# A decoder block on one core: spreading the norms' inverse roots, halving seven accumulating loads, moving two value products

## The chip, the core and the metric

The kernel runs on one core of one Trainium2 chip. The metric is the device time of one execution in microseconds, the median of several runs. A core has five engines that work side by side: TensorE (PE) for matrix products, VectorE (DVE), ScalarE (ACT) and GpSimd (POOL) for work on elements, and SyncE (SP), which here only issues DMAs. Each engine takes its own instructions strictly in order. The loading of a product's stationary operand is shown as an engine of its own, PEld. Data lies in an on-chip memory of 128 partitions; products are written into an accumulation memory, of which this kernel uses eight banks of 128 x 512 fp32.

## What is computed

One decoder block on 512 positions of 1024 channels, in fp32 (cut to what matters here):

```python
def rmsnorm(x, g):
    return x * lax.rsqrt(jnp.mean(x * x, axis=-1, keepdims=True) + EPS) * g

h = rmsnorm(x, norm1_g)
a_b, a_c, a_x, q, kc, vc, ksl, vsl, kwn, vwn, g_nsa, g_merge = split(h @ w_in)
y_a = a_b * causal_dwconv(a_c * a_x, conv_a_w)          # short gated convolution, 512 channels
y_b = nsa(rope(rmsnorm(q)), ...)                        # 8 heads, 2 key groups, 4 blocks of 128 queries
gm = sigmoid(g_merge)                                   # 2 x 1024 columns
x = x + (gm[..., :1024] * (y_a @ w_a_out) + gm[..., 1024:] * (y_b @ w_b_out)) @ w_o
h = rmsnorm(x, norm2_g)
gu = h @ w_ffn_in                                       # 2 x 2816 columns
x = x + (silu(causal_dwconv(gu[..., :2816]) + b) * gu[..., 2816:]) @ w_ffn_out
```

`nsa` is attention with three branches (compressed, selected and window keys), each with its own softmax and gate.

## The kernel before

**Layout.** Channels lie on partitions and the 512 positions along the free axis. A product of 1024 input channels is a chain of products over eight tiles of 128 channels, into one bank.

**Split products.** Every large product is made of three: an operand is cast to fp32r (`hi`) and the remainder kept in a second fp32r tile (`lo`). `dense` (L431) first walks over the channel tiles with hi times hi (L434) and hi weight times lo input (L435), and then a second time over them with the lo weight times the hi input (L437). So for eight tiles there are sixteen "hi" products and, behind them, eight "lo" products; the lo half of the weight is not needed before the seventeenth.

**Weights.** `load_w` (L136) fetches a weight tile of 128 x 1024 (512 KB) through SP into `raw`; ACT casts it to `hi`. The remainder is made in one of three ways. By DVE or POOL it is a subtraction (L147). By "dma" (`dma_split`, L168) ACT writes the negated cast into `lo` (L171), and POOL then issues a DMA that fetches the same weights a second time and adds them to `lo` on the way (L172). `conv_tile` (L776) makes the short convolution's three projections for four channel tiles, twelve loads; seven of them go by "dma". The tile is `wl_a` in the trace. The feed-forward part loads its tiles the same way: `wl_s` (512 KB), `tl` (256 KB), and `wl_d` (512 KB, in pieces).

**Norms.** `row_scales` (L395) makes the mean square of every position as a column per 128 positions, POOL takes the power -1/2 (`r_n`, 128 x 4), and PE spreads it over all partitions (`pr_n`, one bank), from where ACT copies it to `rb_n`. For norm 1 DVE builds a diagonal matrix `dg_n` for each of the four groups of positions and PE multiplies it by a tile of ones, four fp32 products of 128 columns (L412). For norm 2 the column itself is spread against the identity, again four fp32 products (L416).

**Attention.** `attend(pt_, g, qt)` handles one of two key groups `g` and one of four query blocks `qt`; the blocks go from `qt` 3 down to 0, each with group 0 and then group 1. Score products (`sc`, L659 and L660) go to three rotating banks; DVE takes the maximum, ACT the exponential with its sum (L713, an ACTIVATE and a read of the accumulator), and four scaled tiles `e` are turned by a DMA to DRAM (`td_e`) and one back (`tn_e`). Then ACT casts a key tile's part (`ph`, L743), POOL makes the remainder (L744), and PE multiplies the values by both (L746, L751) into `po`. The first product of a block, key tile 0 of branch 1, opens `po`.

**Gates.** `gate_tile` (L799) is a `dense` of the gate weights into `pg`; there are sixteen of them, and they are woven between the attention's products. Tiles are loaded with POOL's subtraction.

**Order.** The instructions are written in program order and then ordered on each engine by a planner that simulates the engines. `behind(later, earlier)` (L226) gives it one ordering condition between two instructions, with no wait of its own on the chip. Engine queues are then fixed.

## Time and profile before

| what | value |
|---|---|
| time, median of 3 runs | 698.46 us (697.29 to 698.58) |
| the profiled execution's own time | 699.54 us |
| its span, first to last instruction | 697.8 us |
| granted TensorE clock over the span | 1.000 of full speed |
| PE busy | 690.3 us, 99% |
| weight loads (PEld) busy | 615.4 us, 88% |
| DVE busy | 509.2 us, 73% |
| ACT busy | 436.7 us, 63% |
| POOL busy | 245.1 us, 35% |
| chain that ended last, by engine | PE 87%, DMA 6%, ACT 2%, POOL 2% |

The profile is of one execution. 1.74 us of its time lie outside the span. Times in rows are counted from the span's start. A product's busy time is modelled as longer than the distance between two starts, since products overlap; distances between starts show the rate. In a row, the bracket gives the idle time of that engine just before and what ended it.

### The profile page before, as it was taken

The page shows a single profiled execution, that of the slowest core. Times are in us where ns is not written, and L with a number is a line of the kernel's source. Part 1 is how long each engine was busy: PE and PEld are TensorE (multiplying, and loading weights), DVE is VectorE, ACT ScalarE, POOL GpSimd, SP SyncE. Part 2 cuts the span into 40 slices and gives each one's busy share as a digit, 9 for nine tenths or more (in the row PEclk, how much of TensorE's full clock was granted, in tenths as well). Part 3 has the DMA queues.
Part 4 walks back from the last instruction along what each step waited for, and adds up shares of the span by engine and source line. Part 5 has one row for each costly group of instructions (what it writes and reads, how often), then busy time and mean ns, then how long its engine had stood idle before and what let it go on. Part 6 is the DMA issues. An engine that isn't in the chain of part 4 may idle for free.

```text
span 697.8 us, 11271 instructions
## 1 busy us (share of the span) xinstructions
PE 690.3 (99%) x4123; PEld 615.4 (88%) x4123; DVE 509.2 (73%) x890; ACT 436.7 (63%) x776; POOL 245.1 (35%) x240
## 2 busy tenths in 40 slices
PE   9999999999999999999999999999999999999997
PEld 8999878878888887888889999999999999999986
DVE  6987975766576646376887999888787777877544
ACT  7635754768898877534776776666466665556530
POOL 4151432467888867552012221211112221112110
PEclk9999999999999999999999999999999999999999
DMA  7333686576776555573587977978977979875665
GB/s 264 116 97 121 159 185 142 143 249 203 250 225 214 172 175 151 179 244 100 141 194 169 234 179 190 224 178 200 221 173 173 213 179 213 184 175 108 133 138 151
DMA packets 56615, 124.87 MB, mean 179 GB/s; under 512 B 5232, under 2 KB 20976, under 8 KB 56560
## 3 DMA queue, kind: packets, MB, share of 16 engines
q1 hardware_dynamic: 35648, 79.39, 35.2%
q0 software_dynamic: 13840, 32.51, 27.4%
q10 hardware_dynamic: 7072, 12.26, 5.7%
q8 instruction: 32, 0.52, 0.3%
q14 instruction: 23, 0.19, 0.1%
HBM read 111.55 MB, written 12.58 MB: 178 GB/s over the span
## 4 chain that ended last, share of the span: by engine, by line
PE 87%; DMA 6%; ACT 2%; POOL 2%; issue 1%; DVE 1%; SPq 0%; POOLq 0%; ACTq 0%
PE p L435 10%; PE p L434 10%; PE p L437 10%; PE pdn L435 6%; PE pdn L434 6%; PE pdn L437 6%; PE pg L434 3%; PE pg L435 3%; PE pg L437 3%; DMA tn_e<-td_e 2%; PE po L435 2%; PE po L434 2%; PE po L437 2%; DMA wl_a<-in_w_a_dram 2%; PE pa L437 2%; PE pa L434 2%
## 5 line engine op out<-in xcount | busy, mean ns | idle before, releaser
L434 PE MATMUL p<-xf_h,sh 128*128 128x256 f32 x336 | 80.9, 276 | 0.0
L435 PE MATMUL p<-xf_l,sh 128*128 128x256 f32 x336 | 80.8, 276 | 0.0
L172 POOL DMA_DIRECT2D wl_s<-in_w_ff_dram x22 | 19.4, 883 | 165.4 <-ACT wl_s L171 151.5
L435 PE MATMUL pdn<-al,wh_d 128*128 128x512 f32 (+1 forms) x176 | 68.5, 389 | 0.0
L434 PE MATMUL pdn<-ah,wh_d 128*128 128x512 f32 (+1 forms) x176 | 68.2, 389 | 0.0
L164 ACT ACTIVATE sh<-s 128x1024 fp32r<-128x1024 f32 x44 | 46.4, 1056 | 27.5 <-PE p L435 26.6
L434 PEld LDWEIGHTS p<-xf_h,sh 128*128 128x128 f32 x336 | 63.1, 188 | 0.1
L435 PEld LDWEIGHTS p<-xf_l,sh 128*128 128x128 f32 x336 | 63.1, 188 | 0.1
L165 DVE TENSOR_TENSOR sl<-s,sh 128x1024 fp32r<-128x1024 f32 x44 | 53.5, 1217 | 10.7 <-ACT sh L164 10.7
L170 ACT ACTIVATE wh_s<-wr_s 128x1024 fp32r<-128x1024 f32 x22 | 23.3, 1060 | 57.1 <-PE pdn L435 53.4
L744 POOL TENSOR_TENSOR tn_e<-tn_e,ph 128x512 fp32r<-128x512 f32 x40 | 51.2, 1297 | 16.8 <-ACT ph L743 16.7
L172 POOL DMA_DIRECT2D wl_d<-in_w_dn_dram x22 | 26.4, 1200 | 74.7 <-ACT wl_d L171 73.5
L437 PE MATMUL p<-xf_h,sl 128*128 128x256 f32 x336 | 52.3, 276 | 0.0
L434 PE MATMUL pg<-xg_h,wh_g 128*128 128x512 f32 x128 | 50.2, 392 | 0.0
L435 PE MATMUL pg<-xg_l,wh_g 128*128 128x512 f32 x128 | 50.1, 392 | 0.0
L437 PE MATMUL pdn<-ah,wl_d 128*128 128x512 f32 (+1 forms) x176 | 47.5, 388 | 0.0
L437 PEld LDWEIGHTS p<-xf_h,sl 128*128 128x128 f32 x336 | 44.8, 188 | 0.2
L1098 DVE TENSOR_TENSOR x<-x,pdn 128x512 f32<-128x512 f32 x47 | 32.0, 681 | 16.6 <-PE pdn L437 16.0
L147 POOL TENSOR_TENSOR wl_g<-wr_g,wh_g 128x1024 fp32r<-128x1024 f32 x16 | 38.5, 2407 | 10.3 <-ACT wh_g L145 10.2
L435 PE MATMUL p<-xf_l,wh_s 128*128 128x256 f32 x168 | 40.4, 276 | 0.0
L434 PE MATMUL p<-xf_h,wh_s 128*128 128x256 f32 x168 | 40.4, 277 | 0.0
L437 PEld LDWEIGHTS pdn<-ah,wl_d 128*128 128x128 f32 x176 | 33.0, 188 | 6.8
(367 smaller groups left out, 2096.7 us busy)
## 6 DMA issues: line engine op xcount, KB each, us to landing
wr_s<-in_w_ff_dram SPq DMA_DIRECT2D x44, 512.0 KB, 5.4
wl_s<-in_w_ff_dram POOLq DMA_DIRECT2D x22, 512.0 KB, 7.7
wr_d<-in_w_dn_dram ACTq DMA_DIRECT2D x22, 512.0 KB, 8.0
wl_d<-in_w_dn_dram POOLq DMA_DIRECT2D x22, 512.0 KB, 9.2
wr_g<-in_w_gate_dram SPq DMA_DIRECT2D x16, 512.0 KB, 4.2
wr_a<-in_w_a_dram SPq DMA_DIRECT2D x12, 512.0 KB, 3.8
tl<-in_w_ff_dram POOLq DMA_DIRECT2D x22, 256.0 KB, 7.9
td_e<-e SPq DMA_DIRECT2D x16, 256.0 KB, 4.6
```

The lines of the kernel that those rows point to most:

```text
L147: e.tensor_sub(lo[:, 0:n], raw[:, 0:n], hi[:, 0:n].bitcast(F32))
L164: hi = nc.scalar.activation(h, v, AF.Copy)
L165: nc.vector.tensor_sub(l, v, h.bitcast(F32))
L170: nc.scalar.activation(h, raw, AF.Copy)
L172: nc.gpsimd.dma_start(l if dst is None else dst, src, accum_op=ALU.add)
L434: nc.tensor.matmul(acc, wh, xh, start=first and i == 0, stop=False)
L435: nc.tensor.matmul(acc, wh, xl, start=False, stop=False)
L437: nc.tensor.matmul(acc, wl, xh, start=False, stop=last and i == len(units) - 1)
L744: nc.gpsimd.tensor_sub(pl, pt, ph.bitcast(F32))
L1098: nc.vector.tensor_add(xj, xj, acc)
```

## The change

Three things are changed.

1. **Norms.** In both norms the root is split into an fp32r part and a remainder (`rs`, DVE: a cast and a subtraction of 128 x 4). DVE builds two rows of diagonal matrices, 128 x 512 each, and PE multiplies a tile of ones by each in one 512-column fp32r product, the second added to the first in the bank. For norm 2 this happens after the feed-forward part's pool has been opened, in a buffer that later holds `cv`.
2. **Convolution weights.** The accumulating DMA of the seven "dma" loads is issued as two, for columns 0 to 511 (channel tiles 0 to 3) and 512 to 1023 (tiles 4 to 7).
3. **Value products.** The first value product of (group 0, block 3) is put behind the seventh product of gate tile 0, and that of (0, 0) behind the eleventh product of gate tile 13. For this, `dense` returns its hi products, and the products are remembered by name.

```diff
@@ load_w
         if by == "dma":
-            dma_split(hi[:, 0:n], lo[:, 0:n], raw[:, 0:n], src)
+            nc.scalar.activation(hi[:, 0:n], raw[:, 0:n], AF.Copy)
+            nc.scalar.activation(lo[:, 0:n], raw[:, 0:n], AF.Copy, scale=-1.0)
+            for c in (slice(0, n // 2), slice(n // 2, n)):
+                nc.gpsimd.dma_start(lo[:, c], src[:, c], accum_op=ALU.add)
@@ row_scales
-        if dg is not None:
-            nc.vector.tensor_tensor(dg, ident[:, None, :].to_broadcast([P, NT, P]), r[:, :, None].to_broadcast([P, NT, P]),
-                                    op=ALU.mult)
-            for t in range(NT):
-                rows = nc.tensor.matmul(pr[:, t * P:(t + 1) * P], ones, dg[:, t, :], start=True, stop=True)
-        else:
-            for t in range(NT):
-
-                rows = nc.tensor.matmul(pr[:, t * P:(t + 1) * P], r[:, t:t + 1].to_broadcast([P, P]), ident, start=True,
-                                        stop=True)
+        rs = sb.tile([P, 2, NT], F32R, name=f"rs_{name}", tag=f"rs_{name}")
+        nc.vector.tensor_copy(rs[:, 0], r)
+        nc.vector.tensor_sub(rs[:, 1], r, rs[:, 0].bitcast(F32))
+        for i in range(2):
+            nc.vector.tensor_tensor(dg[:, i].rearrange("p (t c) -> p t c", t=NT), ident[:, None, :].to_broadcast([P, NT, P]),
+                                    rs[:, i].bitcast(F32)[:, :, None].to_broadcast([P, NT, P]), op=ALU.mult)
+        for i in range(2):
+            rows = nc.tensor.matmul(pr, ones.bitcast(F32R), dg[:, i], start=i == 0, stop=i == 1)
@@ norm 1
-    r1, r1b, _ = row_scales((sq_sum[0][:, 0],), "n1", d_bank, w_tmp("dg_n1", (NT, P)))
+    dg1 = pp.tile([P, TOKC], F32R, name="dg_n1", tag="w4", bufs=NW4)[:, 0:2 * S]
+    r1, r1b, _ = row_scales((sq_sum[0][:, 0],), "n1", d_bank, dg1.rearrange("p (i s) -> p i s", i=2))
@@ dense
+        ops = []
...
-            nc.tensor.matmul(acc, wh, xh, start=first and i == 0, stop=False)
-            nc.tensor.matmul(acc, wh, xl, start=False, stop=False)
+            ops.append(nc.tensor.matmul(acc, wh, xh, start=first and i == 0, stop=False))
+            ops.append(nc.tensor.matmul(acc, wh, xl, start=False, stop=False))
...
+        return ops
+
+    gate_ops, value_op = {}, {}
@@ attend
-                nc.tensor.matmul(acc4, w, ph, start=kt == 0 and br == 1, stop=False)
+                hi = nc.tensor.matmul(acc4, w, ph, start=kt == 0 and br == 1, stop=False)
+                if kt == 0 and br == 1:
+                    value_op[g, qt] = hi
@@ gate_tile
-        dense(acc, w_units(w, xg_h, xg_l, KD))
+        gate_ops[j] = dense(acc, w_units(w, xg_h, xg_l, KD))
@@ after the gates and the mixing
+    for step, j, n in (((0, 3), 0, 6), ((0, 0), 13, 10),):
+        behind(value_op[step], gate_ops[j][n])
@@ norm 2
-    _, r2b, (sums2, rows2) = row_scales((sq2,), "n2", d_bank, None)
...
+    dg2 = pf.tile([P, 2, S], F32R, name="dg_n2", tag="cv", bufs=1)
+    _, r2b, _ = row_scales((sq2,), "n2", d_bank, dg2)
```

How the engines' orders differ is shown at three places. A row there is the kernel's line, the instruction, what it writes and reads, and its size, with a count where it repeats. Lines of the changed kernel are three to twelve higher.

PE at norm 1, before; `pj_s` and `pj_o` are the banks of the token projections, 384 columns each:

```order
L266 MATMUL pj_s_413<-wh_t_447,xg_h 128x384
L267 MATMUL pj_s_413<-wh_t_447,xg_l 128x384
L412 MATMUL pr_n_306<-dg_n_305,ones 128x128 x4
L268 MATMUL pj_s_413<-wl_t_448,xg_h 128x384
L266 MATMUL pj_s_414<-wh_t_447,xg_h 128x384
L267 MATMUL pj_s_414<-wh_t_447,xg_l 128x384
L268 MATMUL pj_s_414<-wl_t_448,xg_h 128x384
```

The same place after:

```order
L270 MATMUL pj_s_415<-wh_t_449,xg_l 128x384
L271 MATMUL pj_s_415<-wl_t_450,xg_h 128x384
L418 MATMUL pr_n_306<-dg_n_305,ones 128x512
L269 MATMUL pj_s_416<-wh_t_449,xg_h 128x384
L270 MATMUL pj_s_416<-wh_t_449,xg_l 128x384
L271 MATMUL pj_s_416<-wl_t_450,xg_h 128x384
L269 MATMUL pj_o_417<-wh_t_449,xg_h 128x384
L270 MATMUL pj_o_417<-wh_t_449,xg_l 128x384
L418 MATMUL pr_n_306<-dg_n_305,ones 128x512
L271 MATMUL pj_o_417<-wl_t_450,xg_h 128x384
L269 MATMUL pj_s_414<-wh_t_449,xg_h 128x384
```

The four products in a row have become two single ones, the second one five projection products behind the first.

PE at the end of the convolution's last lo products (`pa`), where the first value product of (0, 3) stood, before; `pg` is gate tile 0 and `sc` the scores:

```order
L437 MATMUL pa_2460<-xg_h,wl_a_2456 128x512 x8
L746 MATMUL po_1025<-ph_1067,v_t 128x512
L434 MATMUL pg_2495<-xg_h,wh_g_2490 128x512
L435 MATMUL pg_2495<-xg_l,wh_g_2490 128x512
L434 MATMUL pg_2495<-xg_h,wh_g_2490 128x512
L435 MATMUL pg_2495<-xg_l,wh_g_2490 128x512
L434 MATMUL pg_2495<-xg_h,wh_g_2490 128x512
L435 MATMUL pg_2495<-xg_l,wh_g_2490 128x512
L659 MATMUL sc_1247<-kk,qT_825 128x512
L660 MATMUL sc_1247<-kk,qT_825 128x512
L434 MATMUL pg_2495<-xg_h,wh_g_2490 128x512
```

After:

```order
L440 MATMUL pa_2469<-xg_h,wl_a_2465 128x512 x8
L437 MATMUL pg_2504<-xg_h,wh_g_2499 128x512
L438 MATMUL pg_2504<-xg_l,wh_g_2499 128x512
L437 MATMUL pg_2504<-xg_h,wh_g_2499 128x512
L438 MATMUL pg_2504<-xg_l,wh_g_2499 128x512
L437 MATMUL pg_2504<-xg_h,wh_g_2499 128x512
L438 MATMUL pg_2504<-xg_l,wh_g_2499 128x512
L437 MATMUL pg_2504<-xg_h,wh_g_2499 128x512
L752 MATMUL po_1027<-ph_1069,v_t 128x512
L665 MATMUL sc_1249<-kk,qT_827 128x512
L666 MATMUL sc_1249<-kk,qT_827 128x512
L759 MATMUL po_1027<-tn_e_1028_1062,v_t 128x512
```

The value product has moved behind seven gate products, and the score products, which had six gate products between the value product and them, follow it directly.

PE at gate tile 13 (`pg`), where the first value product of (0, 0) stands, before:

```order
L434 MATMUL pg_3158<-xg_h,wh_g_3153 128x512
L435 MATMUL pg_3158<-xg_l,wh_g_3153 128x512
L434 MATMUL pg_3158<-xg_h,wh_g_3153 128x512
L435 MATMUL pg_3158<-xg_l,wh_g_3153 128x512
L434 MATMUL pg_3158<-xg_h,wh_g_3153 128x512
L435 MATMUL pg_3158<-xg_l,wh_g_3153 128x512
L746 MATMUL po_1888<-ph_1936,v_t 128x512
L434 MATMUL pg_3158<-xg_h,wh_g_3153 128x512
```

After:

```order
L437 MATMUL pg_3167<-xg_h,wh_g_3162 128x512
L438 MATMUL pg_3167<-xg_l,wh_g_3162 128x512
L437 MATMUL pg_3167<-xg_h,wh_g_3162 128x512
L438 MATMUL pg_3167<-xg_l,wh_g_3162 128x512
L437 MATMUL pg_3167<-xg_h,wh_g_3162 128x512
L438 MATMUL pg_3167<-xg_l,wh_g_3162 128x512
L437 MATMUL pg_3167<-xg_h,wh_g_3162 128x512
L438 MATMUL pg_3167<-xg_l,wh_g_3162 128x512
L437 MATMUL pg_3167<-xg_h,wh_g_3162 128x512
L438 MATMUL pg_3167<-xg_l,wh_g_3162 128x512
L437 MATMUL pg_3167<-xg_h,wh_g_3162 128x512
L752 MATMUL po_1890<-ph_1938,v_t 128x512
```

It has moved five gate products back.

## Rows read from the trace of the kernel before

**Rows 1.** The page, part 1: busy us of each engine, share of the span, instructions.

```profile
PE 690.3 (99%) x4123; PEld 615.4 (88%) x4123; DVE 509.2 (73%) x890; ACT 436.7 (63%) x776; POOL 245.1 (35%) x240
```

**Rows 2.** The waits of PE, longest first: total us, times, longest us.

```profile
PE po L746 <- ACT ph L743: 1.8, 2, 1.4
```

**Rows 3.** The waits of PE's weight loads, same columns.

```profile
PEld pa L437 <- DMA wl_a<-in_w_a_dram: 1.5, 2, 1.3
```

**Rows 4.** Timeline of all engines at norm 1: start us, us, engine, instruction, [idle before].

```profile
29.62 0.69 DVE L409 TENSOR_TENSOR dg_n<-ident,r_n 128x512 f32<-128x512 f32 x1 [0.86 <-POOL r_n L391]
...
34.31 1.05 PE L412 MATMUL pr_n<-dg_n,ones 128*128 128x128 f32 x8
...
35.37 0.33 PE L266 MATMUL pj_s<-wh_t,xg_h 128*128 128x384 f32 x1
```

**Rows 5.** The same at norm 2.

```profile
369.79 0.15 DVE L403 TENSOR_SCALAR ms_n<-pr_n 128x4 f32<-128x4 f32 x1
...
370.03 1.03 POOL L391 TENSOR_TENSOR r_n<-ms_n,mhalf 128x4 f32<-128x4 f32 x1
...
372.49 0.69 DVE L1016 TENSOR_TENSOR c<-p,p 128x512 f32<-128x512 f32 x1 [2.55 <-ACT p L1038]
...
373.82 1.05 PE L416 MATMUL pr_n<-ident,r_n 128*128 128x128 f32 x8
...
374.84 0.28 PE L435 MATMUL p<-xf_l,wh_s 128*128 128x256 f32 x1
```

**Rows 6.** Timeline of PE at the second accumulating load.

```profile
88.69 0.39 PE L435 MATMUL pa<-xg_l,wh_a 128*128 128x512 f32 x1
...
89.60 0.39 PE L435 MATMUL pa<-xg_l,wh_a 128*128 128x512 f32 x1
90.84 1.65 PE L437 MATMUL pa<-xg_h,wl_a 128*128 128x512 f32 x6 [0.85 <-DMA wl_a<-in_w_a_dram]
```

**Rows 7.** Tiles `wl_a`, `wl_s`, `wl_d`, `tl`, in this order: wait before issue, landing, issue.

```profile
  ACT wl_a L171: 14.1, 5
...
DMA to landing us min/median/max: 5.3/7.7/12.3
...
DMA to landing us min/median/max: 6.2/9.2/12.0
...
L172 POOL DMA_DIRECT2D tl<-in_w_ff_dram x22: 839/854/1074, 335.3 to 631.0; - x22
...
DMA to landing us min/median/max: 3.7/7.9/11.7
```

**Rows 8.** Timeline of all engines at the first value product of (0, 3).

```profile
144.11 1.97 PE L437 MATMUL pa<-xg_h,wl_a 128*128 128x512 f32 x8
...
146.76 1.15 ACT L743 ACTIVATE ph<-tn_e 128x512 fp32r<-128x512 f32 x2 [6.05 <-DMA tn_e<-td_e]
...
147.44 0.50 PE L746 MATMUL po<-ph,v_t 128*128 128x512 f32 x1 [1.35 <-ACT ph L743]
...
147.77 0.39 PE L434 MATMUL pg<-xg_h,wh_g 128*128 128x512 f32 x1
...
148.38 0.19 ACT L713 ACTIVATION_READ_ACCUMULATOR e<-sc,mx 128x1 f32 x1
```

**Rows 9.** The same further on, where ACT and PE next wait.

```profile
165.90 0.58 ACT L713 ACTIVATE e<-sc,mx 128x384 f32<-128x384 f32 x1 [2.47 <-DMA td_e<-e]
...
171.51 0.19 PEld L659 LDWEIGHTS sc<-kk,qT 128*128 128x128 f32 x1 [0.25 <-ACT e L713]
```

**Rows 10.** The same at the first value product of (0, 0).

```profile
275.93 0.39 PE L435 MATMUL pg<-xg_l,wh_g 128*128 128x512 f32 x1
...
276.78 0.50 PE L746 MATMUL po<-ph,v_t 128*128 128x512 f32 x1 [0.47 <-ACT ph L743]
```

**Rows 11.** The same at the first value product of (1, 0).

```profile
282.89 0.63 ACT L743 ACTIVATE ph<-tn_e 128x512 fp32r<-128x512 f32 x1 [3.97 <-DMA tn_e<-td_e]
...
283.77 0.39 PE L746 MATMUL po<-ph,v_t 128*128 128x512 f32 x1
```

## The prediction

> **What bounds the kernel now.** The first line of the page comes first: TensorE (PE) is busy for 690.3 us, 99% of the span [rows 1]. So only three things can move the end: products that are no longer made, moments in which PE stands still, and new such moments. The waits of PE and of its weight loads (PEld) are therefore read next. They are few. PE waited 1.8 us in two places for the cast `ph` ahead of a value product (L746) [rows 2], and PEld 1.5 us in two places for the accumulating DMA of the convolution's low weight halves `wl_a` (L172) [rows 3]. The change touches these places and the two norms. It is a matter of tenths of a microsecond, and 0.2% of the time, about what a measurement of this kernel can tell from no change, is 1.4 us.
>
> **The yardstick.** In an unbroken row PE starts a 512-column product every 0.228 us (from 88.69 to 89.60 is four of them) [rows 6]. After a stall the first product is followed later, 0.33 us from start to start (147.44 to 147.77) [rows 8], so a stall costs about 0.1 us beyond the time that PE stood still.
>
> **Norms.** In the first norm the spreading products `pr_n` start at 34.31, one 384-column product follows, and the next is at 35.37 [rows 4]. That product takes 0.17 us (three quarters of 0.228), so the spreading costs 1.06 - 0.17 = 0.89. In the second norm it is 373.82 to 374.84 with one 256-column product (0.12) between: 0.90 us [rows 5]. The trace counts eight passes for the four fp32 products. Two 512-column fp32r products take their place, 2 x 0.228 = 0.46 us, each a product like its neighbours. Saved: 0.43 and 0.44, together **0.87 us**.
>
> What feeds them is more work on VectorE (DVE): a cast and a subtraction of 128 x 4 (0.15 us each, as `ms_n`) and a second multiplication of 128 x 512 (0.69) [rows 4, 5]. In norm 2 GpSimd (POOL) has the root at 370.03 + 1.03 = 371.06, and DVE is idle for 2.55 us up to 372.49 [rows 5]. The new chain of 0.3 + 1.4 = 1.7 us ends at 372.8. It fits the idle time but for 0.3 us, by which the sums `c` behind it start later; PE's next products into those banks come later than that. In norm 1 the multiplication was made by 29.62 + 0.69 = 30.31 and PE took it at 34.31 [rows 4], so 1.0 us more hides in those 4.0; casts and splits queued behind it on DVE come 1.0 us later, and neither list of waits has PE wait for one [rows 2, 3]. I cost the chain at nothing; without that cover it is up to 1.0 us.
>
> **The convolution's accumulating DMAs.** Seven loads of 512 KB become fourteen of 256 KB. At the second load PE started its last hi product at 89.60, would have gone on at 89.83, and did at 90.84, when the load had landed [rows 6]: 1.01 us lost, and 0.1 after it. Now half one need only serve four lo products. A 256 KB DMA of the same queue (`tl`) lands in 3.7 us at best where 512 KB (`wl_s`) takes 5.3; in the median it is 7.9 against 7.7 [rows 7]. So half one lands between 1.6 us earlier and 0.2 later than the whole did. No other large accumulating load is under way here, so I take the former, about 89.2: PE goes on at 89.83 and has made four by 90.74. Then it wants half two, which is issued one issue time later (854 ns, `tl` [rows 7]). If it travels like half one it lands at 90.80 + 0.85 - 1.6 = 90.05, and all of 1.1 us is gained. If it goes as `wl_d` does, whose 512 KB are rows of 2 KB like those of the halves (least 6.2 against 5.3, median 9.2 against 7.7 [rows 7]), it lands 0.9 to 1.5 us after the old time, at 91.7 to 92.3. PE used to come to its fifth lo product at 90.84 + 0.91 = 91.75, so the gain is then 0 to -0.6. I take 0.5 us late, near the middle of -0.75 and 1.5: at 91.30, a gain of **0.4**, with 1.1 and -0.6 as its ends. The other wait of [rows 3] is 1.5 - 1.3 = 0.2 us: gain **0.1** (0.2 to -0.4). Nobody waits for the five other loads. POOL pays seven issues more, but had waited 14.1 us for casts ahead of five of these loads [rows 7], and that hides them.
>
> The Trainium skill (DMA: Bandwidth & Descriptors, section "Anatomy of one DMA — SWDGE (gpsimd) path") speaks against halves: it gives such a DMA a fixed 2.0 us plus its bytes at 436 GB/s, so that halving 512 KB saves 0.6 us of 3.2. The trace agrees with neither: 1.6 between the least landings, and 5.3 for the whole [rows 7]. By that page half one would land at 90.2 and half two at 90.80 + 0.85 - 0.6 = 91.05, an estimated gain of 0.6 here where I took 0.4; the total would be 0.2 lower.
>
> **The first value product of (group 0, block 3).** PE's eight lo products start from 144.11, so the next product could start at 145.93. It is the value product, at 147.44, with the next at 147.77 [rows 8]: 1.51 + 0.1 = 1.6 us lost. Its cast could begin only when the turned probabilities had landed, at 146.76 [rows 8]. Now seven gate products stand ahead: 145.93 + 7 x 0.228 = 147.53, just past the cast. That stall is gone. But a score product, which stood behind six gate products, now comes right behind the value product, at 147.75. There are three score banks, and the one it needs is read by an exponential whose accumulator read ends at 148.38 + 0.19 = 148.57 [rows 8]. PE stands still again for 0.8 us and 0.1 more, and 0.7 of the 1.6 us is left. This has a second gate: ScalarE (ACT) works on from 146.76, a time that a DMA set, until it next waits for a DMA, at 165.90 [rows 9]; PE runs into ACT at 171.51, where it waits 0.25 us already [rows 9]. A PE that is 0.7 us early waits 0.7 longer there. I take **0** for this move, with 1.6 as its good end; it has no bad one, as PE has the same work either way and the cast is no later.
>
> **The first value product of (0, 0).** PE's next start would have been 275.93 + 0.23 = 276.16 and was 276.78 [rows 10]: with 0.1 after it, 0.7 us lost. Five more gate products, 1.1 us, cover it. The next block's value product then comes 0.7 us earlier than 283.77, at 283.05; but its cast, after a DMA for which ACT waited 3.97 us, ends at 282.89 + 0.63 = 283.52 [rows 11]. Of the 0.7 us 0.5 + 0.1 is given back: gain **0.1** (to 0.7, if that DMA moves forward with PE).
>
> The planner's order shifts in other places too (score and convolution products about 100 us; casts and loads of three feed-forward tiles). PE waits for none of these before [rows 2, 3]; I take 0, with 0.3 us to either side.
>
> **Sum.** 0.87 + 0.4 + 0.1 + 0 + 0.1 = 1.5 us. Against the profiled execution, whose 697.8 of span and 1.74 around it make 699.54, that is 698.0. That execution lies 1.08 us above the median, 698.46; for the median it is 698.46 - 1.5 = **696.9 us**.
>
> **Rivals.** (B) The stalls' gains pass whole: 0.87 + 1.1 + 0.2 + 0.7, and 0.7 of (0, 3): 3.6 us, 694.9. For it: PE has few waits further on in which to give it back [rows 2, 3], and ACT's chain may come earlier with PE. Against: ACT's start is a DMA's landing, and PE waits at 171.51 [rows 8, 9]. (C) The halves gain nothing, since rows of 2 KB go as slowly as those of `wl_d`, and the value products only move their waits: the norms alone, 0.87, with 0 to 0.3 lost elsewhere: 697.8. For it: the medians of [rows 7]. (D) Slower: half two lands a time d after the old whole. At both tight loads PE then waits at the fifth lo product, d - 0.91 each. With 3 us (the worst `tl` took 4.0 more than the median `wl_s` [rows 7]) that is 2 x 2.1 = 4.2 lost against the 1.0 that norms and (0, 0) give: 3.2 us slower, 701.7. It makes the kernel slower by over 0.2% from d = 2.1, where 2 x 1.2 is 1.0 + 1.4. Against it: only two of seven loads are waited for at all, one of them by 0.2 us [rows 3], so the queue is not crowded here.
>
> **Chances.** Forecast 0.48, with its own range 696.2 to 697.7; B 0.22; C 0.22; D 0.08. The line of 0.2% lies at 697.06: two thirds of the forecast's cases and all of B are faster, 0.32 + 0.22 = 0.54; D is slower, 0.08; the rest, 0.38, is no change. The range that leaves out D and half of B is 695.2 to 698.4.
>
> **What would show it.** In the changed trace: two `pr_n` products of a normal product's length in each norm; PE's idle time at about 90 gone or halved, and standing ahead of the fifth lo product; no wait for `ph` at 147, but one of some 0.8 us at a score product right after; a longer wait at about 171, which shows the gain given back, and one at about 283. I would be wrong with no score wait at 148 and an earlier chain on ACT (B), with an idle time at 91 as long as the old (C), or with PE waiting for second halves by over 1 us (D).

## The result and the profile after

The change makes the kernel slower. The changed kernel takes **704.06 us** (median, 704.0 to 705.03) against 698.46 (697.29 to 698.94): a ratio of 1.0083, 95% interval 1.0072 to 1.0095, or 5.6 us. Forecast were 696.9 us and a range up to 698.4. The profiled execution has a span of 702.2 us where that of before had 697.8. Two executions of the experiments, at a granted clock of 0.557, took 1157 and 1158 us and are left out of all medians and ratios below.

Nothing in the lists of waits shows the loss. First the page's line of the engines' busy times after, which answers [rows 1]:

```profile
PE 697.4 (99%) x4111; PEld 622.6 (89%) x4111; DVE 512.8 (73%) x897; ACT 436.5 (62%) x776; POOL 248.0 (35%) x247
```

All waits of PE after, the answer to [rows 2] (who waited for what, us in total, times, longest; this one lies at the kernel's start and was there before):

```profile
PE wu L198 <- POOL ones L193: 1.1, 1, 1.1
```

The longest waits of PEld behind the start, the answer to [rows 3]:

```profile
PEld sc L665 <- ACT e L719: 0.8, 3, 0.4
PEld po L759 <- POOL tn_e L750: 0.8, 2, 0.4
PEld po L752 <- ACT ph L749: 0.6, 2, 0.3
```

PE is busy 7.1 us longer than the 690.3 of [rows 1]. PE's waits for `ph` and its weight loads' waits for `wl_a` are gone. So PE neither stands still nor has more to do: it does the same work more slowly. One has to ask at which products. The count of products in a stretch of the feed-forward part tells it (columns: stretch, its length, busy time of PE, PEld, DVE, ACT and POOL with the number of instructions, granted clock, DMA share, GB/s), of before:

```profile
450.00:666.00 216.00, 216.00 (x1564) 202.59 (x1564) 167.80 (x232) 129.02 (x169) 41.04 (x42) 1.00 0.78 179
```

and of after:

```profile
450.00:666.00 216.00, 216.00 (x1517) 202.16 (x1517) 166.74 (x230) 126.92 (x167) 40.21 (x40) 1.00 0.77 176
```

In both, PE is busy all of the 216 us at a granted clock of 1.00 (the level of 2.4 GHz); after, it starts 47 products fewer. The groups of products of that part (busy us, mean ns of one) show which kind is slower. Before:

```profile
L434 PE MATMUL p<-xf_h,sh 128*128 128x256 f32 x336 | 80.9, 276 | 0.0
L434 PE MATMUL p<-xf_h,wh_s 128*128 128x256 f32 x168 | 40.4, 277 | 0.0
L434 PE MATMUL pdn<-ah,wh_d 128*128 128x512 f32 (+1 forms) x176 | 68.2, 389 | 0.0
```

After:

```profile
L437 PE MATMUL p<-xf_h,sh 128*128 128x256 f32 x336 | 82.9, 280 | 0.0
L437 PE MATMUL p<-xf_h,wh_s 128*128 128x256 f32 x168 | 41.7, 281 | 0.0
L437 PE MATMUL pdn<-ah,wh_d 128*128 128x512 f32 (+1 forms) x176 | 68.4, 390 | 0.0
```

The 512-column products `pdn` are as they were; both their operands lie on the right-hand side and were not moved. The 256-column products of `sh` and `wh_s` take 4 ns more each. The starts show the pace directly, in PE's timeline at 500 us (start, us, instruction), before:

```profile
500.12 0.28 PE L434 MATMUL p<-xf_h,sh 128*128 128x256 f32 x1
...
500.69 0.28 PE L435 MATMUL p<-xf_l,sh 128*128 128x256 f32 x1
```

and after:

```profile
500.26 0.28 PE L438 MATMUL p<-xf_l,sh 128*128 128x256 f32 x1
...
500.85 0.28 PE L437 MATMUL p<-xf_h,sh 128*128 128x256 f32 x1
```

From the first to the last of these are five steps (four rows are left out in each): 0.57 us before and 0.59 after, 114 ns a product against 118. In the median from 455 us on it is 113 against 118. Over all 1,891 products of 256 columns the times from start to start sum to 217.24 us before and 223.58 after: **6.3 us**.

Comparing the starts of the same products gives the balance. Minus means earlier than in the profiled execution of before; that execution lies 1.08 us above its median, so all leads in this document look that much larger than they are against the median. The place of this surplus can be seen: eight kernels of the experiments below, those that only move tiles of the kernel before, have its order on every engine and leave the value products where they were, and yet in their traces PE is 0.9 to 1.7 us further ahead behind the first value product of (0, 3).

| from | to | what happens there | lead after it |
|---|---|---|---|
| 0 | 21 us | start of the kernel | +0.22 |
| 21 | 45 | norm 1 | -0.14 |
| 45 | 93 | second `wl_a` load | -1.15 |
| 93 | 118 | sixth `wl_a` load | -1.34 |
| 118 | 160 | around the value product of (0, 3) | -2.5 |
| 160 | 196 | given back ahead of scores | -1.6 |
| 196 | 281 | value product of (0, 0) | -2.2 |
| 281 | 380 | norm 2 | -2.0 |
| 385 | 667 | 256-column products | **+4.3** |

The gains are there, 2 us of them and about 1 against the median. The last row turns them into a loss.

What differs there without a changed instruction is the place of the data. The new code makes two tiles `rs_n1` and `rs_n2` of 32 bytes a partition in the pool `sb`, the first pool on the left-hand side of the on-chip memory. All that lies behind them is moved by 64 bytes: the normed inputs `xf_h`, `xf_l` and the weights `th`, `tl`, `sh`, `sl`. The weights `wh_s`, `wl_s` of the right-hand side stay.

### The profile page after: what moved, and what is told of

It is laid out like the page before. It is cut to its first block, busy times and chain, and to the rows that moved or that the text cites. A ratio compares the mean times of both kernels' runs of the same rounds, so it can differ in the third digit from the quotient of the medians.

```text
span 702.2 us, 11268 instructions
## 1 busy us (share of the span) xinstructions
PE 697.4 (99%) x4111; PEld 622.6 (89%) x4111; DVE 512.8 (73%) x897; ACT 436.5 (62%) x776; POOL 248.0 (35%) x247
## 4 chain that ended last, share of the span: by engine, by line
PE 90%; ACT 3%; DMA 2%; DVE 1%; POOL 1%; issue 1%; SPq 0%; ACTq 0%; POOLq 0%
PE p L438 10%; PE p L437 10%; PE p L440 10%; PE pdn L438 6%; PE pdn L437 6%; PE pdn L440 6%; PE pg L437 4%; PE pg L438 3%; PE pg L440 3%; PE pa L438 2%; PE pa L437 2%; PE pa L440 2%; PE po L437 2%; PE po L438 2%; PE po L440 2%; PE pj_s L269 2%
## 5 line engine op out<-in xcount | busy, mean ns | idle before, releaser
L438 PE MATMUL p<-xf_l,sh 128*128 128x256 f32 x336 | 82.9, 280 | 0.0
L437 PE MATMUL p<-xf_h,sh 128*128 128x256 f32 x336 | 82.9, 280 | 0.0
L438 PE MATMUL p<-xf_l,wh_s 128*128 128x256 f32 x168 | 42.0, 281 | 0.0
L175 POOL DMA_DIRECT2D tl<-in_w_ff_dram x22 | 19.7, 894 | 56.1 <-ACT tl L174 46.5
```

The costliest lines, as they stand in the source:

```text
L175: nc.gpsimd.dma_start(l if dst is None else dst, src, accum_op=ALU.add)
L437: ops.append(nc.tensor.matmul(acc, wh, xh, start=first and i == 0, stop=False))
L438: ops.append(nc.tensor.matmul(acc, wh, xl, start=False, stop=False))
```

## The experiments on the place of the tiles

Below, "apart" is the distance from the start of a product's inputs (`xf_h`, `xf_l`) to that of its weights, within 128 bytes (what is left of it when divided by 128). Before: `th` 0, all others 64. After: `th` 0, `tl`, `sh`, `sl` 64, but `wh_s`, `wl_s` 0.

**The change with its roots in unused columns of existing tiles**, so that nothing moves; the order of PE, ACT, POOL and SP is that of the changed kernel.

```diff
...
-        rs = sb.tile([P, 2, NT], F32R, name=f"rs_{name}", tag=f"rs_{name}")
+        rs = [t[:, NT:2 * NT].bitcast(F32R) for t in (r8, ms8)]
...
```

> The changed kernel with the same instructions in the same order on every engine; only the two 32-byte tiles for the split root are gone: their values lie in unused columns of the tiles that hold the mean and the root, so no tile to the left of the attention's pools moves by 64 bytes. Theory P (place): in the changed kernel 256-column products start every 118 ns instead of 113 because their operands lie 64 bytes further; then this kernel has 113 to 114 ns again from about 445 us on, keeps the 2.0 us that the change had gained by 400 us, and takes 696.0 to 697.0 us. Theory O (order): the feed-forward part's changed order, or the new place of the buffers cv and c on the other side, sets the slower pace; then 118 ns stays, and the time is 704.

Measured: 697.4 us, ratio 0.9988 (0.9977 to 0.9998). The pace is 113 ns again. The 6 us are the tiles, not the edits.

**The kernel before with two unused tiles of 32 bytes**, its order unchanged.

```diff
+        sb.tile([P, 8], F32, name=f"pad_{name}", tag=f"pad_{name}")
```

> The kernel before with two unused tiles of 32 bytes where the change puts its split root; no instruction is added or moved, but all tiles on the left side lie 64 bytes further, as in the changed kernel. Theory P: 256-column products every 118 ns throughout; some 1,500 of the 1,891 at +4 to +5 ns is 6 to 7 us, so 704 to 706. Theory O: 698.5, within 0.3.

Measured: 705.01 us (the median of three), 1.0097 (1.0078 to 1.0116), 118 ns to the end. 64 bytes that nobody uses do all the harm. With the run before this settles where the loss comes from. What about the place is harmful was the next question.

**Only `tl`, `sh`, `sl` moved by 64 bytes.**

```diff
-    const([P, 48], "gap_w", F32, pw)
+    const([P, 64], "gap_w", F32, pw)
```

> The kernel before with the gap ahead of the feed-forward weights' tiles 64 bytes larger: only the stationary operands made on the left (th, tl, sh, sl) and the sums lie 64 bytes further; the inputs xf, and the weights wh_s and wl_s on the other side, stay. Theory P in the form that the stationary operand's place counts: products with sh, sl and tl at 118 ns, those with wh_s and wl_s at 113: about 1,200 x 5 ns, 702 to 705. In the form that the place of the input xf counts: no change, 698.5. Theory O: 698.5.

**Only the inputs and `th` moved by 64 bytes.**

```diff
-    const([P, 80], "gap_x", F32, px)
+    const([P, 96], "gap_x", F32, px)
...
-    const([P, 48], "gap_w", F32, pw)
+    const([P, 32], "gap_w", F32, pw)
```

> The kernel before with the gap ahead of the inputs xf 64 bytes larger and the gap behind them 64 bytes smaller: only xf (and the first two cast tiles th) lie 64 bytes further, all other weights stay. Theory P in the form that the input's place counts: all 256-column products at 118 to 119 ns, 704 to 706. In the form that the stationary operand's place counts: 698.5. Theory O: 698.5.

Measured: 704.6 us (1.0092, 1.0072 to 1.0113) and 707.19 (1.0120, 1.0103 to 1.0138). Either move is enough. In the first, products of moved and unmoved weights stand side by side; its groups:

```profile
L434 PE MATMUL p<-xf_h,sh 128*128 128x256 f32 x336 | 84.4, 283 | 0.0
L434 PE MATMUL p<-xf_h,wh_s 128*128 128x256 f32 x168 | 40.4, 277 | 0.0
```

The moved `sh` starts every 120 ns, the unmoved `wh_s` every 113, on the same inputs. So the pace changes from product to product with the operands; it is not the whole engine that is slowed.

**Only `th` moved**, by letting it stand behind the gap.

```diff
-    pw.tile([P, D // 2], F32R, name="th_", tag="th", bufs=2)
     const([P, 48], "gap_w", F32, pw)
+    pw.tile([P, D // 2], F32R, name="th_", tag="th", bufs=2)
```

> The kernel before with the gap of 192 bytes ahead of the tiles th instead of behind them: only th lies 192 bytes further, at the same remainder of 512 bytes as sh, sl, tl, wh_s and wl_s; no instruction is added or moved. Theory P (a product of 256 columns takes 113 ns with the operands' remainders of 288 and 480, and 117 to 121 with others): the 168 products with th, at 117 to 121 ns before, take 113 to 114, 0.7 to 1.2 us faster: 697.3 to 697.8. Without it: 698.5, products unchanged.

Measured: 703.66 us, 1.0087 (1.0069 to 1.0105). I expected a gain: `th`, the only weights 0 apart before, are slow at 116 to 121 ns. Instead all products go at 117 to 120 ns, `sh` too (280 ns in its group), whose own operands had not been moved. My theory that the places of a product's own operands alone make it fast or slow fell with this.

**Inputs and left-hand weights moved by 128 bytes.**

```diff
-    const([P, 80], "gap_x", F32, px)
+    const([P, 112], "gap_x", F32, px)
```

> The kernel before with the gap ahead of xf 128 bytes larger: xf and all weights made on the left lie 128 bytes further, at remainders of 416 and 96 of 512; wh_s and wl_s stay at 480. If what counts is the place within 128 bytes (32 for the inputs, 96 for the weights, as before): 113 ns everywhere, 698.5. If it is the place within 256 or 512 bytes, or the distance between particular tiles: products at 117 to 121 ns in part, 701 to 706.

Measured: 698.58 us, 1.0010 (0.9998 to 1.0021), 113 ns. 128 bytes do no harm.

**The changed kernel as it is, with 64 bytes more**, so that inputs and weights are 128 bytes from their old places.

```diff
-    const([P, 80], "gap_x", F32, px)
+    const([P, 96], "gap_x", F32, px)
```

> The changed kernel whole, its two new 32-byte tiles where they are, with 64 bytes more in the gap ahead of the normed inputs (80 to 96 float32 columns): the inputs and the parts th are then 128 bytes from their old places (416 of 512), the other left-hand weights too (96 of 512). Theory P128 (the pace of the 256-column products goes by the places of their operands within 128 bytes): the products start every 113 ns again from 450 us on, and the time is that of the change at its old places, 697.4 us (696.5 to 698.5). If only the exact old places, or some other thing that the 128-byte kernel shared with before, make the pace: 118 to 120 ns to the end and 703 to 705 us.

Measured: **697.03 us**, 0.9982 (0.9973 to 0.9992). One constant turns the slower kernel into a faster one. Its stretch in the feed-forward part has 1,563 products again:

```profile
450.00:666.00 216.00, 216.00 (x1563) 202.69 (x1563) 168.13 (x234) 128.82 (x169) 41.66 (x42) 1.00 0.79 181
```

and its group of `sh` products the old duration:

```profile
L437 PE MATMUL p<-xf_h,sh 128*128 128x256 f32 x336 | 80.4, 276 | 0.0
```

**Inputs and left-hand weights moved by 32 bytes** (`gap_x` 88).

```diff
-    const([P, 80], "gap_x", F32, px)
+    const([P, 88], "gap_x", F32, px)
```

> The kernel before with 32 bytes more in the gap ahead of the normed inputs: inputs and th at 64 within 128 bytes, the other left-hand weights at 0, the right-hand ones at 96. Theory P128 does not say which places are fast; if whatever differs from the places of before (32, 32, 96, 96) is slow: 703 to 706 us and 117 to 120 ns. If the pace is lost only where the inputs and the weights that they meet stand the same way within 64 bytes (a shift of 64 moves one onto the other, of 32 does not): 698.5 us and 113 ns.

Measured: 702.6 us, 1.0060 (1.0047 to 1.0073). Neither expectation: `sh` and `sl`, moved together with the inputs and still 64 apart, go at 113; `wh_s`, now 32 apart, at 115 to 125. Their groups:

```profile
L434 PE MATMUL p<-xf_h,sh 128*128 128x256 f32 x336 | 81.0, 277 | 0.0
L435 PE MATMUL p<-xf_l,wh_s 128*128 128x256 f32 x168 | 42.2, 284 | 0.0
```

This pointed to the distance between a product's operands. The last two kernels were made to test that.

**Everything moved by 64 bytes, every distance kept**: before, with 64 bytes ahead of the inputs, and 64 on the right-hand side.

```diff
         w = ring_w(w_bo[i], f"bo{i}")
+        if i == 0:
+            const([P, 16], "gap_r", F32, wf)
...
-    const([P, 80], "gap_x", F32, px)
+    const([P, 96], "gap_x", F32, px)
```

> The kernel before, its order unchanged, with the inputs, th and the other left-hand weights 64 bytes further, as in the changed kernel, and by a 64-byte gap on the right-hand side also wh_s and wl_s moved by 64 bytes (places within 128 bytes: inputs 96, th 96, left weights 32, right weights 32). Theory D (it is the distance between the inputs and the weights of a product that counts, not where they lie: 64 bytes apart as before can go at 113 ns, th with distance 0 stays as it was): 113 ns from 450 us on and 698.0 to 699.0 us. Theory of places (inputs or weights in the wrong half of 128 bytes are slow): 117 to 120 ns and 703 to 706 us.

**Only the right-hand weights moved by 64 bytes**: the same without the second piece, so that `wh_s`, `wl_s` are 0 apart.

> The kernel before with only wh_s and wl_s (and what lies below them on the right-hand side) moved by 64 bytes: right weights at 32 as the inputs are, th at 32, the other left weights at 96. Theory D: wh_s and wl_s, at distance 0, go at 117 to 121 ns; the left weights keep their distance of 64 and go at 113 ns, or at 117 to 118 where they follow the right ones; 504 products lose 4 to 7 ns each, 2 to 3.5 us: 700.5 to 702.5 us, up to 705 if the left ones go along. If the right weights' place does not matter: 698.5 us.

Measured: 698.84 us (1.0007, 0.9998 to 1.0016) and 705.75 (1.0099, 1.0084 to 1.0114). The groups where all is moved:

```profile
L434 PE MATMUL p<-xf_h,sh 128*128 128x256 f32 x336 | 80.9, 277 | 0.0
L434 PE MATMUL p<-xf_h,wh_s 128*128 128x256 f32 x168 | 40.4, 277 | 0.0
```

and where only the right-hand weights are:

```profile
L434 PE MATMUL p<-xf_h,sh 128*128 128x256 f32 x336 | 83.0, 279 | 0.0
L434 PE MATMUL p<-xf_h,wh_s 128*128 128x256 f32 x168 | 41.6, 281 | 0.0
```

In the first every operand of these products lies 64 bytes from its old place, the left-hand ones where the slow changed kernel has them, and the pace is that of before. The second has all left-hand tiles in their old places, but the distances of the changed kernel, and has its pace, group by group. It is the distance that counts. All kernels together (bytes apart, and ns from start to start after 455 us, from the 5th to the 95th of a hundred, worked out from the traces):

| kernels | `th` | `tl` | `sh`, `sl` | `wh_s`, `wl_s` |
|---|---|---|---|---|
| before; all moved by 64; moved by 128; change and 64 more | 0 apart: 116 to 121 | 64: 113 | 64: 113 | 64: 113 |
| after; two unused tiles; right weights by 64 | 0: 117 to 121 | 64: 113 to 118 | 64: 117 to 119 | 0: 113 to 122 |
| left weights by 64 | 0: 116 to 121 | 0: 120 to 121 | 0: 120 | 64: 113 |
| inputs by 64 | 0: 117 to 120 | 0: 112 to 124 | 0: 115 to 122 | 0: 115 to 122 |
| `th` alone | 64: 117 to 120 | 64: 117 to 119 | 64: 117 to 119 | 64: 117 to 119 |
| inputs and left weights by 32 | 0: 117 to 121 | 64: 113 to 124 | 64: 113 | 32: 115 to 125 |

Steady at 113 ns are only products 64 apart; at 0 and 32 apart the medians are 117 ns or more. But 64 apart is not enough: most such products go at one of two steady paces, 113 or 117 to 118. What ran ahead of them seems to decide. In the trace of before the feed-forward part begins at 118, with all its operands 64 apart, until the first `th`, 0 apart, and goes at 113 behind it. Two groups of eight products in its PE timeline, `sh` from 380.25 and `wh_s` from 383.07, each up to the next row:

```profile
380.25 0.28 PE L434 MATMUL p<-xf_h,sh 128*128 128x256 f32 x1
...
381.20 0.63 PE L437 MATMUL p<-xf_h,sl 128*128 128x256 f32 x4
381.66 0.28 PE L434 MATMUL p<-xf_h,th 128*128 128x256 f32 x1
...
383.07 0.28 PE L434 MATMUL p<-xf_h,wh_s 128*128 128x256 f32 x1
...
383.97 0.62 PE L437 MATMUL p<-xf_h,wl_s 128*128 128x256 f32 x4
```

The eight of `sh` take 0.95 us, 119 ns each, and the eight of `wh_s` 0.90, 113 each. Behind the first 512-column products, at 409.5 us, the pace is 118 again, until the next `th` at 415.5. That fits the run that surprised me: with `th` moved to 64, nothing is 0 apart, and no product ever takes up 113. But `th` is not the whole of it: where all is moved by 64, or inputs and left-hand weights by 128, only the second `th` brings 113, and where norm 2 is that of the change and the places are the old ones, the part begins at 113. From 455 us on, behind left-hand weights at 0 and behind right-hand ones at 32 products at 64 take up 113, and behind `wh_s`, `wl_s` at 0 they take up 118. This is read from the traces and no run was made to test it; why some products hand on one pace and some the other is not shown.

For 512-column products the distance works the other way. `pmb`, a product ahead of norm 2, has its inputs on the left-hand side and its weights on the right, 0 apart before and 64 after. Before:

```profile
L434 PE MATMUL pmb<-y,wh_bo 128*128 128x512 f32 x32 | 12.4, 389 | 0.0
```

After:

```profile
L437 PE MATMUL pmb<-y,wh_bo 128*128 128x512 f32 x32 | 12.6, 393 | 0.0
```

In every kernel of this section these products take 389 ns where they are 0 apart and 393 where they are 64; over the 96 products of `pmb` that is some 0.4 us.

## The experiments on the three edits

They leave all tiles of these products in their old places. They are pieces of the change, and norms keep their roots in unused columns, as in the first experiment; the diffs show what marks each.

**The norms alone**, both as in the change.

```diff
...
+        rs = [t[:, NT:2 * NT].bitcast(F32R) for t in (r8, ms8)]
...
+            rows = nc.tensor.matmul(pr, ones.bitcast(F32R), dg[:, i], start=i == 0, stop=i == 1)
```

> The kernel before with the two norms of the change alone, the split root in unused columns as in the first experiment, so that nothing lies 64 bytes further. Changing norm 2 also lets the planner put the feed-forward tiles 4 to 6 in another order; in the first experiment PE then stood 1.2 us for a cast `ah` at about 419. Theory A (that order costs more than norm 2 saves): 0.4 gained at norm 1, up to 0.45 at norm 2, 1.2 to 1.4 lost at 419: 0.1 to 0.6 us slower than before, 698.5 to 699. Theory B (the prediction's term: the norms give 0.87 and the order nothing): 697.5.

Measured: 698.09 us, 0.9993 (0.9982 to 1.0004), a gain of 0.4 that can't be told from none. The products gain what was forecast. But the diagonals of norm 2 on DVE give the feed-forward part another order, and new waits come with it: from 400 to 445 us 1.0 us of the lead is lost, in several short waits here, of which PE's for `ah` has 0.2. In the changed kernel with 64 bytes more it is one wait. PE's longest wait there:

```profile
PE pdn L437 <- ACT ah L167: 1.2, 1, 1.2
```

PE's timeline at that place:

```profile
419.57 0.74 PE L437 MATMUL pdn<-ah,wh_d 128*128 128x512 f32 x2 [1.21 <-ACT ah L167]
```

and ACT's, with two casts of weights left out between:

```profile
416.90 0.63 ACT L173 ACTIVATE th<-wr_s 128x512 fp32r<-128x512 f32 x1 [3.94 <-DMA wr_s<-in_w_ff_dram]
...
418.91 1.14 ACT L167 ACTIVATE ah<-up 128x512 fp32r<-128x512 f32 x2
```

ACT waits 3.94 us for a weight load, then casts three weights, and only then `ah`, on which PE stands. In the changed kernel as it was this wait doesn't show: its PE is late enough by then.

**The halves alone.**

```diff
-            dma_split(hi[:, 0:n], lo[:, 0:n], raw[:, 0:n], src)
+            nc.scalar.activation(hi[:, 0:n], raw[:, 0:n], AF.Copy)
+            nc.scalar.activation(lo[:, 0:n], raw[:, 0:n], AF.Copy, scale=-1.0)
+            for c in (slice(0, n // 2), slice(n // 2, n)):
+                nc.gpsimd.dma_start(lo[:, c], src[:, c], accum_op=ALU.add)
```

> The kernel before with the seven accumulating DMAs in halves and nothing else. Theory A (the second half lands in time, as in the changed kernel, where PE did not stop at the second load): 1.1 us gained at 90 and 0.15 at 116, all of it passed on to the end: 697.1, and no wait of PE for wl_a. Theory B (the prediction: the second half lands 0.5 us late): 0.4 and 0.1, 697.9, with PE idle for some 0.5 us ahead of the fifth lo product at about 91.

Measured: 699.69 us, 1.0018 (1.0009 to 1.0026): slower by 1.2, where a gain was expected. At 118 us the kernel is 1.6 us ahead, by 282 us 0.7 behind.

**The value products alone.**

```diff
+    for step, j, n in (((0, 3), 0, 6), ((0, 0), 13, 10),):
+        behind(value_op[step], gate_ops[j][n])
```

> The kernel before with the two value products moved and nothing else; the planner changes no other engine's order. Theory A: the (0, 3) move gives 1.5 us at 147 of which 0.7 to 1.0 is given back at waits for ACT at 171 and 195, and the (0, 0) move gives 0.7, of which 0 to 0.6 is given back at 283: 0.6 to 1.4 in all, 697.1 to 697.9. Theory B (the prediction): PE stands 0.8 us at the score product behind the value product, and all but 0.1 us is given back: 698.3.

Measured: 698.35 us, 0.9997 (0.9988 to 1.0006). At (0, 3) PE comes out 1.65 us further ahead and gives back 0.7 by 195; at (0, 0) it gains 0.5 and gives it back at a gap of 0.59 us at 282. But the 1.65 are not the move's: the eight kernels that have the order of before gain 0.9 to 1.7 us at (0, 3) without it. One of them is the kernel with 128 bytes more; its ACT and PE there:

```profile
145.13 1.15 ACT L743 ACTIVATE ph<-tn_e 128x512 fp32r<-128x512 f32 x2 [4.38 <-DMA tn_e<-td_e]
```

```profile
145.81 0.50 PE L746 MATMUL po<-ph,v_t 128*128 128x512 f32 x1
```

The load `tn_e` that the cast waits for took 7.8 us from issue to landing in the profiled execution of before, but 5.6 to 6.9 in those eight, and PE waited 0 to 0.4 us where [rows 8] has 1.35. So the large wait is one of that execution, and the move has little to take away.

**Halves and value products, no norms.**

```diff
+            for c in (slice(0, n // 2), slice(n // 2, n)):
+                nc.gpsimd.dma_start(lo[:, c], src[:, c], accum_op=ALU.add)
...
+        behind(value_op[step], gate_ops[j][n])
```

> The kernel before with the halves and the two moved value products, both norms as before; the feed-forward order and every place are those of before. Theory A (the halves' 1.3 us were lost in the first attention block because PE arrived early at a value product that could not start; with gate products ahead of it the gain passes): 0.4 us, norm 1's part, less than the fastest version so far, 697.3 to 697.9. Theory B (the halves alone cost 1.2 us by something of their own, such as their issue time on POOL): halves and value products together lie at +1.2 - 0.1, 699.6.

Measured: 700.05 us, 1.0023 (1.0009 to 1.0038), slower again. It left no trace that can be read, so the same kernel was run and profiled once more.

> The halves and the two moved value products, no norms, at the old places: the kernel that took 700.11 us and left no profile that can be read. Theory H (the attention stage gives the lead back at waits for the activations that scatter and rotate the scores, as with the halves alone): the time is again 699.6 to 700.6 us, the lead at 118 us is 1.0 to 1.5 us, and gaps of TensorE between 144 and 290 us sum to 1.5 us or more above those of before. Rival P2 (the 256-column products of the last 250 us run slower again): the lead at 290 us is 2 us and is lost by 600 us. Rival: the former time was that chip's, and it is 697.0 to 698.3 us.

Measured: 699.82 us, 1.0019 (1.0011 to 1.0028), so the time repeats. The profiled execution took 699.14. At 160 us its lead is 3.0 us, at 172 it is 0.7. Where the 2.3 us go is shown by SP's DMA queue: the store of the exponentials `td_e`, and `tn_e`, whose issue waits for the store to have landed. In the changed kernel the step takes 163.95 - 157.57 = 6.4 us:

```profile
157.57 2.87 SPq L658 DMA_DIRECT2D td_e<-e  x4
163.95 0.38 SPq L660 DMA_DIRECT2D tn_e<-td_e  x1
```

With halves and value products it takes 165.07 - 157.14 = 7.9:

```profile
157.14 2.86 SPq L659 DMA_DIRECT2D td_e<-e  x4
165.07 0.38 SPq L661 DMA_DIRECT2D tn_e<-td_e  x1
```

Behind it, in ACT's timeline of that kernel, and then in PE's:

```profile
165.10 0.58 ACT L720 ACTIVATE e<-sc,mx 128x384 f32<-128x384 f32 x1 [4.09 <-DMA td_e<-e]
```

```profile
165.82 0.44 PE L666 MATMUL sc<-kk,qT 128*128 128x384 f32 x1 [1.32 <-ACT e L720]
```

And two stretches of it, with the columns as above:

```profile
161.00:163.00 2.00, 2.00 (x11) 1.60 (x10) 1.69 (x4) 0.01 (x1) 2.00 (x4) 1.00 0.85 219
163.00:164.00 1.00, 1.00 (x6) 0.84 (x5) 0.00 (x0) 0.00 (x0) 1.00 (x1) 1.00 0.01 2
```

From 163 us on the DMA engines are idle (share 0.01), yet the store counts as landed only at 165.07. ACT, and with it the scores, begin 1.5 us late. With the halves alone the step takes 7.96 us; before it takes 6.31, with the norms 6.20, with the value products 6.34, and in the kernel that follows 6.35. So most of the loss is placed: it is this store, in both kernels that have the halves without the first norm, each seen in one execution. Why it ends late only there stays open. Theory H was right in the mechanism; by 290 us 1.0 us of the lead was lost in the profiled execution, less than the 1.5 that it expected, and the median lies another 0.7 higher. The theory that the pace is lost was wrong: it is 113 ns.

**All but norm 2** (the diff is against the whole change): norm 1, halves, value products; the feed-forward part keeps its order.

```diff
-    dg2 = pf.tile([P, 2, S], F32R, name="dg_n2", tag="cv", bufs=1)
-    _, r2b, _ = row_scales((sq2,), "n2", d_bank, dg2)
+    _, r2b, _ = row_scales((sq2,), "n2", d_bank, None)
```

> The changed kernel without its second norm (which is as before) and with the first norm's split root in unused columns: nothing lies 64 bytes further, and the feed-forward part has its old order on every engine. Theory A (place and order are what the change lost): the 2.0 to 2.6 us by which the changed kernel leads at 360 stay to the end, no wait for `ah` at 419: 695.9 to 696.5, faster than both kernels. If something else of the change slowed the feed-forward part, the time is 697.4 or more, as in the first experiment.

Measured: 697.26 us, 0.9979 (0.9970 to 0.9988). The lead of 2.4 us at 287 us is kept to the end.

**All but norm 2, `th` moved, and the first value product of (1, 0) moved too.**

```diff
-    pw.tile([P, D // 2], F32R, name="th_", tag="th", bufs=2)
     const([P, 48], "gap_w", F32, pw)
+    pw.tile([P, D // 2], F32R, name="th_", tag="th", bufs=2)
...
-    for step, j, n in (((0, 3), 0, 6), ((0, 0), 13, 10),):
+    for step, j, n in (((0, 3), 0, 6), ((0, 0), 13, 10), ((1, 0), 14, 9)):
```

> The fastest version so far (all of the change but norm 2, nothing 64 bytes further, 697.3) with th moved as in the run beside it, and with the first value product of (1, 0), for which PE stood 0.87 us at 280, put behind the tenth product of gate tile 14. Expected: 0.7 to 1.2 us less for th, 0.3 to 0.9 for the value product: 695.3 to 696.3. If the value product only moves its wait, as the prediction had it for (0, 3): 696.1 to 696.6.

Measured: 703.24 us, 1.0080 (1.0064 to 1.0095): the move of `th` spoils it as it spoils the kernel before. Therefore once without it, with the last two lines of the diff alone:

> Norm 1, halves and both moved value products with the second norm as before, all at the old places (697.26 us before), and the first value product of (1,0) behind the tenth gate product of group 14. Theory: the 0.87 us gap ahead of (1,0) at 280 us becomes small and the lead is kept to the end, 696.4 to 696.9 us. Rival: the score product or the inputs of (1,0) wait 0.5 to 0.9 us right behind it, as they did behind (0,0) with the value products alone, and the time stays at 697.1 to 697.4 us.

Measured: **696.34 us** (695.7 to 697.71), 0.9972 (0.9960 to 0.9983): 2.2 us faster than before, the fastest kernel of this study. Its lead at 290 us is 3.2 us where it was 2.4 without the last move. No wait of PE behind the kernel's start is left in its list but this one of 0.2 us:

```profile
PE pj_s L269 <- DVE xg_h L295: 0.2, 1, 0.2
```

## Why the prediction was wrong

**The step that is missing.** The prediction costs instructions, waits and orders. It takes for granted that an untouched product takes as long as before: the sum has no term for the 1,891 products of 256 columns, and no rival has one. It said that there are only three things that can move the end: products no longer made, moments in which PE stands still, and new such moments. The fourth, the same products at another pace, was worth 6.3 us, more than all terms together. The trace of before shows two paces of such products (119 and 113 ns, in the rows at 380 us above), but not what sets them; the places of the tiles were in the two programs, and differ by 64 bytes.

**Norms, 0.87.** The products are as forecast. PE's timeline of after at norm 1:

```profile
34.82 0.39 PE L418 MATMUL pr_n<-dg_n,ones 128*128 128x512 f32 x1
35.05 0.34 PE L269 MATMUL pj_s<-wh_t,xg_h 128*128 128x384 f32 x1
...
35.95 0.39 PE L418 MATMUL pr_n<-dg_n,ones 128*128 128x512 f32 x1
36.18 0.34 PE L271 MATMUL pj_o<-wl_t,xg_h 128*128 128x384 f32 x1
```

0.23 us each, against the 0.89 for the four in [rows 4]; the lead grows by 0.36 at norm 1 (0.43 forecast), and by about 0.6 at norm 2 where the places are the old ones, of which some 0.2 are the 52 products behind it, which go at 114 ns there and at 118 before. The chain on DVE costs nothing at norm 1. At norm 2 it changes the planner's order, and the waits that come with it take 1.0 to 1.5 us back, 1.2 of them for `ah` in the row above. "I take 0, with 0.3 us to either side" for shifts of the order was too small by a factor of four, since I looked only for waits that were there before.

**Halves, 0.4 + 0.1.** Rival B's end was right: all of 1.1 us and 0.2. In the view of the tile `wl_a` the seven whole loads of before landed in

```profile
DMA to landing us min/median/max: 5.7/7.4/7.9
```

and the fourteen halves of after in

```profile
DMA to landing us min/median/max: 5.4/6.3/7.1
```

PE's timeline of after at the second load:

```profile
89.90 1.98 PE L440 MATMUL pa<-xg_h,wl_a 128*128 128x512 f32 x8
```

The eight lo products of the second load run without a wait (the answer to [rows 6]). The halves land in 6.3 us in the median, sooner than `tl` (7.9) and `wl_d` (9.2) [rows 7], and half two not late as I feared. The halving saved 1.1 us in the median and 0.3 at the least; the 0.6 us estimated from the Trainium skill (DMA: Bandwidth & Descriptors, section "Anatomy of one DMA — SWDGE (gpsimd) path") lie between, though the 3.2 us that it would give for the whole are less than the 5.7 seen. That the halves alone lose all of it again, mostly at a store 70 us later, was no case of mine. What is gained ahead of the attention part goes through it, and there a DMA's landing decides.

**Value product of (0, 3), 0.** The number held by luck. The 1.6 us that it weighs were read from one execution; in eight others with the same order PE waits 0 to 0.4 us there (the run of the value products alone). And the first reason, a wait of the scores, was wrong. ACT's timeline of after:

```profile
144.78 1.15 ACT L749 ACTIVATE ph<-tn_e 128x512 fp32r<-128x512 f32 x2 [4.57 <-DMA tn_e<-td_e]
```

and PE's, in which no score waits:

```profile
146.45 0.40 PE L752 MATMUL po<-ph,v_t 128*128 128x512 f32 x1
146.68 0.47 PE L665 MATMUL sc<-kk,qT 128*128 128x512 f32 x1
146.99 0.40 PE L666 MATMUL sc<-kk,qT 128*128 128x512 f32 x1
```

I had left ACT's cast at 146.76 [rows 8]. It comes 2.0 us earlier: the load `tn_e` is issued at 138.46 where it was 138.96, and takes 6.3 us where it took 7.8. What made it slow in the execution of before stays open. The lead grows by 1.2 us here, as much as without the move; 0.9 are given back by 196, where I expected it, at PE's meeting with ACT [rows 9].

**Value product of (0, 0), 0.1.** Right, by the runs. In the profiled execution of after PE waits at neither this product nor the next block's. But with the value products alone the 0.5 gained are given back at 282, as forecast for the middle case, and in the changed kernel with its roots in unused columns or with 64 bytes more PE stands 0.35 and 0.7 us at the value product of (1, 0).

**In sum** the edits on their own are worth 0.8 to 1.3 us (ratios 0.9988 and 0.9982, 697.4 and 697.03 us), near the forecast 1.5, by errors that cancel: the halves gave 1.2 where 0.5 were forecast, and norm 2's order took 1.0 to 1.5.

## What to carry to other kernels

A new tile, however small, moves everything behind it, so compare the places of the operands of the longest stretches before and after, within 128 bytes, and put new small values into unused columns or pad to 128. When a kernel turns slower and no wait explains it, compare the mean duration of untouched products, or the count of products in a stretch in which PE is always busy, before any wait. A gain ahead of a part whose start is set by a DMA's landing has to be measured behind that part. And a stall that hangs on such a landing should be read from a second execution before it enters a sum.

## What was not expected of the hardware

- The pace of 256-column fp32r products goes by the distance between the inputs' and the weights' places within 128 bytes: a steady 113 ns was only seen at 64, and medians of 117 to 120 at 0 and 32. Products at 64 go at 113 or at 117 to 118, by what ran ahead of them (`th` alone moved: 703.66 us). The 512-column products `pmb` go the other way, 389 ns at 0 and 393 at 64. What in the engine does this stays open.
- A store was seen as landed 2 us after the DMA engines had gone idle (163 to 165.07 us), in two kernels; from its issue this took 7.9 us, and 6.2 to 6.5 in the others.
- The same load of 1 MB, `tn_e`, took 5.6 to 7.8 us in executions with the same order on every engine, and PE waited 0 to 1.35 us for it.
